# One copy of an input matrix read through a strided view instead of loaded, in two buffers: the input stage of an S5 recurrence

## The chip, the cores and the metric

The kernel runs on one core of a Trainium2 chip. The metric is the device time of one execution in microseconds. A core has five engines with a queue of instructions each: PE (matrix products, with PEld for its weight loads), DVE (vector), ACT (scalar functions), POOL (general vector work) and SP, which here issues all DMA transfers. Instructions of one queue run in the order in which they were written down. An instruction that waits holds up all that stand behind it on its engine.

## The reference

The model is a two-layer backbone over 128 context tokens and 2048 sample tokens of width 1024. Layer 0 runs an HGRN2 recurrence and an S5 recurrence side by side between an input and an output projection; layer 1 is a gated short convolution between two projections. What matters here is the input side of S5. For each of 32 groups of 16 channels and each of two directions, a complex diagonal state of 64 numbers is driven by the channels:

```python
bb_re = coef_re[..., None] * b_re - coef_im[..., None] * b_im
bb_im = coef_re[..., None] * b_im + coef_im[..., None] * b_re
bu_re = jnp.einsum('blgs,gps->blgp', useq, bb_re[d])
bu_im = jnp.einsum('blgs,gps->blgp', useq, bb_im[d])
```

and the state follows x_t = lambda x_(t-1) + bu_t.

## The kernel before

The kernel does not step through the tokens one by one. It works on blocks of 16 tokens: `s5_in` builds, for each direction and group, matrices that carry the 16 tokens of a block to the block's share in the state. It multiplies them with the channel inputs, and `s5_scan` then runs the recurrence over the blocks. `s5_out` makes the outputs.

`s5_in` has 8 rounds `r` of 4 groups. A round has two steps, one for each direction `d`. A step loads `pb` (L613: real and imaginary part of B, and beside them the same with the two parts swapped, 4 KB on each of 128 partitions, 512 KB in all). For each half `hh` of the block it loads `pe` (L617: powers of the decay times the coefficient, 2 KB on each partition, 256 KB) and makes the complex product in four instructions: DVE multiplies the real part of `pe` with `pb[:, 0]` into `psi` (L622), POOL multiplies the imaginary part with the swapped `pb[:, 1]` into `ptb` (L623), and DVE subtracts and adds the halves (L624, L625). After both steps PE multiplies the four matrices `psi` with the inputs `su` (L599, four loads of 136 KB in a round) into the PSUM tile `lv` (L633, 32 products in a round, 16 for each step), and ACT and DVE copy `lv` into the state array `sX` (L638, L639).

`pe`, `ptb`, `psi` and `su` have two buffers each, `pb` has one: the next `pb` can be loaded only when both POOL products that read the last one have ended. The source patterns of `pb` and of `pe` have 8 as their outermost size. The loads `su` also begin with 8.

Beside this stage PE works on large input projections (`pj`, L362: three products for each tile of weights, since every factor is split in a high and a low part). Their weights `wraw` come by L339, ACT and DVE or POOL split them (`whi` L342, `wlo` L346), and their outputs go through `zst` (L390, L392, L407) to DRAM.

The order of the instructions of each queue is not written by hand. The program gives each instruction a priority (`s5_in` ranks 500 ahead of what stands beside it), and a planner walks through the program before the run with an estimated duration for each instruction and transfer. Whenever an engine is free in that plan it takes the ready instruction of the highest rank. What comes out is a fixed order on each queue. How many `pj` products stand between two groups of `lv` products thus follows from how long the planner thinks that a step of `s5_in` lasts.

Of the kernel before, what the change touches and what calls it, by code (L numbers as in the profile page):

```python
# [11 lines left out]
F32 = mybir.dt.float32  # L12
# [4 lines left out]
OP = mybir.AluOpType  # L17
# [47 lines left out]
def vw(t, off, dims):  # L65
    return bass.AP(t.tensor, t.offset + off, [list(t.ap[0])] + [list(d) for d in dims])


def raw_ap(t, off, dims):
    return bass.AP(t.tensor, t.offset + off, [list(d) for d in dims])  # L70
# [525 lines left out]
def s5_load_u(nc, g, p, g0):  # L596
    u = p.tile([128, 2, NC8], F32, name="su")
    for j in range(2):
        nc.sync.dma_start(u[:, j], raw_ap(g.u_d, (g0 + j) * 16 * 8 * NC8, [(NC8, 8), (8 * NC8, 16), (1, NC8)]))  # L599
    return u  # L600


def s5_in(nc, g, p, X):

    V, A, T, G = nc.vector, nc.scalar, nc.tensor, nc.gpsimd
    W = WX
    for r in range(8):
        G0 = 4 * r
        us = [s5_load_u(nc, g, p, G0 + 2 * q) for q in range(2)]
        SI = []  # L610
        for d in range(2):
            bt = p.tile([128, 2, 4, 2, 64], F32, name="pb", bufs=1)
            nc.sync.dma_start(bt.rearrange("p a g r q -> p a (g r q)"),  # L613
                              raw_ap(g.I["s5_bt"], d * 16 * 8192 + r * 1024, [(0, 8), (8192, 16), (1, 1024)]))
            for hh in range(2):
                e = p.tile([128, 4, 2, 64], F32, name="pe")
                nc.sync.dma_start(e.rearrange("p g r q -> p g (r q)"),  # L617
                                  raw_ap(g.et_d, ((d * 16 + 8 * (1 - hh)) * 32 + G0) * 128,
                                         [(32 * 128, 8), (0, 16), (1, 512)]))
                si = p.tile([128, 4, 2, 64], F32, name=f"psi{d}{hh}")  # L620
                tb = p.tile([128, 4, 2, 64], F32, name="ptb")
                V.tensor_tensor(si, vw(e, 0, [(128, 4), (0, 2), (1, 64)]), bt[:, 0], op=OP.mult)  # L622
                G.tensor_tensor(tb, vw(e, 64, [(128, 4), (0, 2), (1, 64)]), bt[:, 1], op=OP.mult)  # L623
                V.tensor_tensor(si[:, :, 0], si[:, :, 0], tb[:, :, 0], op=OP.subtract)  # L624
                V.tensor_tensor(si[:, :, 1], si[:, :, 1], tb[:, :, 1], op=OP.add)  # L625
                SI.append(si)
        for q in range(2):
            pr = 2 * r + q
            for j in range(2):
                P = g.ps_l.tile([128, 512], F32, name="lv")  # L630
                for d in range(2):
                    for hh in range(2):
                        T.matmul(out=P[:, d * NC16:(d + 1) * NC16],  # L633
                                 lhsT=SI[2 * d + hh][:, 2 * q + j].rearrange("p r q -> p (r q)"),
                                 rhs=vw(us[q], j * NC8 + hh, [(2, NC16)]), start=(hh == 0), stop=(hh == 1))
                o = slice(64 * j, 64 * j + 64)
                Pv = P[:, :2 * NC16].rearrange("p (d a b) -> p d b a", d=2, b=8)
                A.activation(vw(X[o], pr * W + NG16, [(32 * W - NG16, 2), (NG16, 8), (1, NG16)]), Pv[0:64], AF.Copy)  # L638
                V.tensor_copy(vw(X[o], (16 + pr) * W + NG16, [(32 * W - NG16, 2), (NG16, 8), (1, NG16)]), Pv[64:128])  # L639
# [446 lines left out]
def kernel(ctx: ExitStack, tc: tile.TileContext, I, O, dram=None):  # L1086
# [118 lines left out]
    with tc.tile_pool(name="big0", bufs=1) as b0:  # L1205
        with tc.tile_pool(name="kt", bufs=1) as kt:
# [25 lines left out]
            with tc.tile_pool(name="s5x", bufs=1) as xp:  # L1232
                X = xp.tile([128, 2, 2, 16, WX], F32, name="sX")
                with tc.tile_pool(name="s5i", bufs=2) as p5:
                    with rank(tc, -RI):
                        s5_in(nc, g, p5, X)
                proj_all(nc, g, rest, p0, hs, 1)
                with tc.tile_pool(name="s5s", bufs=2) as p5:
                    with rank(tc, -RC):
                        s5_scan(nc, g, p5, X)  # L1240
                make_h(p1[0])
                with tc.tile_pool(name="s5o", bufs=2) as p5:
                    with rank(tc, -RO):
                        s5_out(nc, g, p5, X)
                nc.sync.dma_start(O["st_s5"], g.xfin)
# [113 lines left out]
def layout(inputs):  # L1359
    a = {k: np.asarray(v) for k, v in inputs.items()}  # L1360
    c = np.ascontiguousarray
    r = {}
    r["x"] = c(np.concatenate([a["x_prompt"][0], a["x_sample"][0]], 0).T)
    r["w_mod"] = c(a["w_mod"].reshape(2, 8, 128, 6, 512).transpose(0, 3, 2, 1, 4))

    def blocks(w, k):
        n = w.shape[1] // 128
        return c(w.reshape(k, 128, n, 128).transpose(2, 1, 0, 3))

    r["w_in_even"] = blocks(a["w_in_even"][0], 8)  # L1370
    r["w_out_even"] = blocks(a["w_out_even"][0], 8)
    r["w_in_odd"] = blocks(a["w_in_odd"][0], 8)
    r["w_out_odd"] = blocks(a["w_out_odd"][0], 8)
    r["w_glu"] = c(a["w_glu"][0].reshape(4, 128, 512).transpose(1, 0, 2))

    def feat(v):
        return v.reshape(-1, 128).T

    pv = np.zeros((128, PVW), np.float32)

    def put(k, v):
        pv[:, PV[k][0]:PV[k][1]] = v

    put("cvec", np.stack([a["c_ctx"], a["c"][0]], -1).reshape(8, 128, 2).transpose(1, 0, 2).reshape(128, 16))
    put("b_mod", np.concatenate([feat(a["b_mod"][l]) for l in range(2)], 1))
    put("norm_g", np.concatenate([feat(a["norm_g"][l]) for l in range(2)], 1))
    put("fin_g", feat(a["final_norm_g"]))
    put("lbl", np.concatenate([feat(a["lb_logits"][l]) for l in range(2)], 1))
    put("hg", feat(a["hgrn_norm_g"][0]))
    put("bglu", feat(a["b_glu"][0]))  # L1390
    put("convw", np.concatenate([feat(a["conv_w"][0, j]) for j in range(3)], 1))
    put("convb", feat(a["conv_b"][0]))
    d = np.zeros((4, 32, 8), np.float32)
    d[:, :16, :] = a["s5_d"][0].reshape(8, 4, 16).transpose(1, 2, 0)
    put("s5d", d.reshape(128, 8))
    r["pv"] = pv
    r["eye"] = np.eye(128, dtype=np.float32)
    e16 = np.zeros((4, 32, 16), np.float32)
    e16[:, :16] = np.eye(16)
    r["eye16"] = e16.reshape(128, 16)  # L1400
    idx = np.arange(32)
    m = np.zeros((4, 32, 6, 32), np.float32)
    m[:, :, 0] = np.eye(32)
    for l in range(5):
        h = 1 << l
        b, t = idx // (2 * h), (idx // h) % 2
        m[:, :, l + 1] = (b[:, None] == b[None]) & (t[:, None] != t[None])
    m = m.reshape(128, 6, 32)
    r["masks"] = m
    r["state_hgrn"] = c(a["state_hgrn"][0, 0].transpose(0, 2, 1, 3).reshape(2, 128, 512))  # L1410
    x0 = np.stack([a["state_s5_re"][0, 0], a["state_s5_im"][0, 0]], 1)
    r["s5_x0"] = c(x0.reshape(2, 2, 16, 2, 64).transpose(3, 4, 0, 1, 2).reshape(128, 2, 2, 16))
    r["s5_lam_re"] = c(a["s5_lam_re"][0].reshape(64, 64))
    r["s5_lam_im"] = c(a["s5_lam_im"][0].reshape(64, 64))
    r["s5_log_dt"] = c(a["s5_log_dt"][0].reshape(64, 1))
    bre, bim = a["s5_b_re"][0], a["s5_b_im"][0]
    cre, cim = a["s5_c_re"][0], a["s5_c_im"][0]
    bt = [np.stack([p, q], 2).transpose(0, 4, 1, 2, 3).reshape(2, 16, 8, 512) for p, q in ((bre, bim), (bim, bre))]
    r["s5_bt"] = c(np.stack(bt, 3))
    br, bi = bre.transpose(2, 0, 1, 3), bim.transpose(2, 0, 1, 3)  # L1420
    r["s5_x1"] = c(np.concatenate([br, bi], 0))
    r["s5_x2"] = c(np.concatenate([bi, br], 0))
    cs = np.stack([cre, cim], 1).transpose(4, 0, 1, 2, 3).reshape(64, 2, 2, 512)
    r["s5_c"] = c(np.concatenate([cs, cs], 0))
    return r
# [25 lines left out]
```

## Time and profile before

| | us |
|---|---|
| median of 3 runs | 2525.39 |
| range of the runs | 2523.67 to 2532.09 |
| the profiled execution, its own time | 2521.9 |
| span of the profile | 2520.1 |
| PE busy | 2336.8 (93%) |
| DVE busy | 1384.5 (55%) |
| ACT busy | 992.5 (39%) |
| POOL busy | 686.9 (27%) |

The profile is of one execution, and its span is 1.8 us shorter than that execution's own time. PE's clock has two levels, 1.2 and 2.4 GHz; the profile gives the mean granted clock of a stretch as a share of the higher one, so 0.81 means that a part of the stretch ran at half speed. Busy shares are means over stages with different limits. The stages can be told apart by time: modulation and the first projections up to 150 us, loads and matrices of `s5_in` beside projections to 250, the rest of `s5_in` to 391, `s5_scan` to 516, then `s5_out`, HGRN2, the output projections and layer 1.

### The profile page before, as it was taken

Reading aid. Unit: us, or ns where it says so; the run is one execution under the profiler, and the core shown is the slowest. Engines: PE = TensorE matmul, PEld = TensorE weight load, DVE = VectorE, ACT = ScalarE, POOL = GpSimd, SP = SyncE. Lnnn points to the kernel's source line nnn. Section 1 sums busy time; section 2 is a strip of 40 time slices with the busy share of each in tenths; the row PEclk is TensorE's granted clock in tenths of the full one; section 3 lists DMA queues with packets and bytes.
Section 4 is the critical chain, followed back from the end, with each engine's and each line's share of the span. In section 5 each row is a group of like instructions: output and inputs, shape, how many; then the busy total and the mean of one; then the engine's idle time right before and its main releaser. Section 6 shows DMA issues by size and latency. Waiting matters only on the chain. (4 is left out here: it accounts for less than half of the span.)

```text
span 2520.1 us, 46630 instructions
## 1 busy us (share of the span) xinstructions
PE 2336.8 (93%) x18452; PEld 2235.7 (89%) x18452; DVE 1384.5 (55%) x2960; ACT 992.5 (39%) x1991; POOL 686.9 (27%) x740
## 2 busy tenths in 40 slices
PE   5999778999989889999898999999999999999997
PEld 3998768998877778979788999999999999899997
DVE  5976648966555886067667652244622244622233
ACT  3544212234455875266444332233422232422221
POOL 0334332232222333133222322223322222322120
PEclk8999889999999989999998999999999999999999
DMA  7577653355565554453896432234321223222221
GB/s 257 149 216 216 172 157 112 117 164 156 146 196 160 156 169 153 153 182 103 249 288 214 135 113 76 76 94 140 97 68 59 65 86 115 71 67 60 67 66 60
DMA packets 277418, 340.16 MB, mean 135 GB/s; under 512 B 79056, under 2 KB 221136, under 8 KB 277072
## 3 DMA queue, kind: packets, MB, share of 16 engines
q1 hardware_dynamic: 277200, 337.18, 44.2%
q8 instruction: 145, 2.38, 0.4%
q14 instruction: 73, 0.60, 0.1%
HBM read 265.18 MB, written 71.94 MB: 134 GB/s over the span
## 5 line engine op out<-in xcount | busy, mean ns | idle before, releaser
L362 PE MATMUL pj<-hhi,whi 128*128 128x384 f32 (+1 forms) x3648 | 1178.1, 333 | 41.4 <-ACT hhi L304 24.0
L362 PE MATMUL pj<-hlo,whi 128*128 128x384 f32 (+1 forms) x3648 | 1179.8, 332 | 9.5 <-DVE hlo L305 7.8
L362 PE MATMUL pj<-hhi,wlo 128*128 128x384 f32 (+1 forms) x3456 | 1142.9, 331 | 0.3 <-DVE wlo L346 0.3
L362 PEld LDWEIGHTS pj<-hhi,whi 128*128 128x128 f32 x3648 | 691.6, 191 | 53.9 <-ACT hhi L304 25.7
L362 PEld LDWEIGHTS pj<-hlo,whi 128*128 128x128 f32 x3648 | 692.2, 191 | 17.0 <-DVE hlo L305 11.9
L362 PEld LDWEIGHTS pj<-hhi,wlo 128*128 128x128 f32 x3456 | 660.6, 191 | 3.8 <-issue 1.6
L346 POOL TENSOR_TENSOR wlo<-wraw,whi 128x256 fp32r<-128x256 f32 x472 | 382.9, 843 | 1017.5 <-ACT whi L342 948.3
L342 ACT ACTIVATE whi<-wraw 128x512 fp32r<-128x512 f32 x472 | 271.7, 623 | 560.9 <-PE pj L362 359.7
L346 DVE TENSOR_TENSOR wlo<-wraw,whi 128x256 fp32r<-128x256 f32 x472 | 191.1, 462 | 102.3 <-ACT whi L342 102.1
L1055 DVE TENSOR_TENSOR ccg<-ccg,pj 128x384 f32<-128x384 f32 (+1 forms) x48 | 25.5, 532 | 248.5 <-PE pj L362 233.0
L828 POOL TENSOR_TENSOR hK<-hK,ht 128x512 f32<-128x512 f32 x68 | 91.7, 1350 | 224.0 <-ACT hMg L812 143.1
L995 DVE SCALAR_TENSOR_TENSOR xr<-pj,mod,xr 128x384 f32<-128x384 f32 (+2 forms) x152 | 77.3, 529 | 135.5 <-PE pj L362 122.9
L304 ACT ACTIVATE hhi<-nsq,mod 128x384 fp32r<-128x384 f32 (+2 forms) x144 | 75.0, 557 | 66.3 <-DVE nsq L302 66.2
L283 DVE TENSOR_TENSOR nac<-nac,nsq 128x384 f32<-128x384 f32 (+1 forms) x112 | 71.7, 641 | 28.3 <-ACT nsq L282 25.8
L830 DVE TENSOR_TENSOR hQ<-hQ,ht 128x512 f32<-128x512 f32 x102 | 78.8, 787 | 14.8 <-PE lv L798 10.8
L623 POOL TENSOR_TENSOR ptb<-pe,pb 128x512 f32<-128x512 f32 x32 | 53.5, 1681 | 115.2 <-DMA pb<-in_s_bt 85.5
L633 PE MATMUL lv<-su,psi 128*128 128x136 f32 x256 | 47.8, 344 | 37.1 <-DVE sX L639 21.3
L305 DVE SCALAR_TENSOR_TENSOR hlo<-nsq,mod,hhi 128x384 fp32r<-128x384 f32 (+2 forms) x144 | 81.3, 591 | 1.0 <-ACT hhi L304 0.9
L282 ACT ACTIVATE nsq<-xr 128x384 f32<-128x384 f32 (+1 forms) x84 | 42.1, 503 | 96.8 <-DVE xr L995 91.3
L633 PEld LDWEIGHTS lv<-su,psi 128*128 128x128 f32 x256 | 43.2, 238 | 41.6 <-DVE sX L639 23.2
L392 ACT ACTIVATE zst<-pj 128x384 f32<-128x384 f32 (+1 forms) x96 | 44.4, 464 | 81.2 <-PE pj L362 49.6
L1075 DVE TENSOR_TENSOR ccs<-ccs,pj 128x384 f32<-128x384 f32 (+1 forms) x48 | 25.3, 528 | 88.8 <-ACT ccs L1074 88.8
(299 smaller groups left out, 2826.6 us busy)
## 6 DMA issues: line engine op xcount, KB each, us to landing
wraw<-in_w_in_odd SPq DMA_DIRECT2D x96, 512.0 KB
wraw<-in_w_in_even SPq DMA_DIRECT2D x92, 512.0 KB
mwm<-in_w_mod SPq DMA_DIRECT2D x64, 256.0 KB
big<-in_x SPq DMA_DIRECT2D x10, 1536.0 KB
wraw<-in_w_out_even SPq DMA_DIRECT2D x24, 512.0 KB
wraw<-in_w_out_odd SPq DMA_DIRECT2D x24, 512.0 KB
su<-u_d SPq DMA_DIRECT2D x64, 136.0 KB
pb<-in_s_bt SPq DMA_DIRECT2D x16, 512.0 KB
```

Of the source, the lines that this page charges most:

```text
L283: e.tensor_tensor(acc, acc, sq[:, :n], op=OP.add)
L304: A.activation(hi[:, k, a:b], raw[:, a:b], AF.Identity, bias=sh)
L305: V.scalar_tensor_tensor(lo[:, k, a:b], raw[:, a:b], sh, hi[:, k, a:b].bitcast(F32), op0=OP.add, op1=OP.subtract)
L342: nc.scalar.activation(hi[:, i:i + ca], raw[:, i:i + ca], AF.Copy)
L346: e.tensor_tensor(lo[:, k], raw[:, k], hi[:, k].bitcast(F32), op=OP.subtract)
L362: nc.tensor.matmul(out=P[:, :n], lhsT=a[:, k, :], rhs=b[:, k, :n], start=(k == 0 and i == 0), stop=(k == kd - 1 and i == 2))
L392: nc.scalar.activation(st[:, :n], P[:, :n], AF.Copy)
L623: G.tensor_tensor(tb, vw(e, 64, [(128, 4), (0, 2), (1, 64)]), bt[:, 1], op=OP.mult)
L633: T.matmul(out=P[:, d * NC16:(d + 1) * NC16], lhsT=SI[2 * d + hh][:, 2 * q + j].rearrange("p r q -> p (r q)"), rhs=vw(us[q], j * NC8 + hh, ...
L828: (G if lvl in KPOOL else V).tensor_tensor(kv, kv, vw(tot, n + 1, [(-n - 1, 2), (2, nb), (0, h)]), op=OP.mult)
L830: V.tensor_tensor(qv, qv, vw(tot, 1, [(n - 1, 2), (2, nb), (0, h)]), op=OP.mult)
L995: nc.vector.scalar_tensor_tensor(x[:, a:e], P[:, a:e], g.mod[l][:, 16 + b, s:s + 1], x[:, a:e], op0=OP.mult, op1=OP.add)
```

## The change

The array in DRAM holds the real and the imaginary part of B once, not twice, and its rows become half as long. The tile `pb` becomes 2 KB on each partition instead of 4 KB, and its DMA carries 256 KB instead of 512 KB. The swapped copy is no longer loaded: POOL's product reads the one copy through a view whose middle step is negative, first the imaginary part (offset 64), then the real part. The argument `bufs=1` goes, so that `pb` takes the two buffers of its pool; the room in SBUF is the same. The number of instructions and of transfers is unchanged.

```diff
-            bt = p.tile([128, 2, 4, 2, 64], F32, name="pb", bufs=1)
-            nc.sync.dma_start(bt.rearrange("p a g r q -> p a (g r q)"),
-                              raw_ap(g.I["s5_bt"], d * 16 * 8192 + r * 1024, [(0, 8), (8192, 16), (1, 1024)]))
+            bt = p.tile([128, 4, 2, 64], F32, name="pb")
+            nc.sync.dma_start(bt.rearrange("p g r q -> p (g r q)"),
+                              raw_ap(g.I["s5_bt"], d * 16 * 4096 + r * 512, [(0, 8), (4096, 16), (1, 512)]))
...
-                V.tensor_tensor(si, vw(e, 0, [(128, 4), (0, 2), (1, 64)]), bt[:, 0], op=OP.mult)
-                G.tensor_tensor(tb, vw(e, 64, [(128, 4), (0, 2), (1, 64)]), bt[:, 1], op=OP.mult)
+                V.tensor_tensor(si, vw(e, 0, [(128, 4), (0, 2), (1, 64)]), bt, op=OP.mult)
+                G.tensor_tensor(tb, vw(e, 64, [(128, 4), (0, 2), (1, 64)]), vw(bt, 64, [(128, 4), (-64, 2), (1, 64)]),
+                                op=OP.mult)
...
-    bt = [np.stack([p, q], 2).transpose(0, 4, 1, 2, 3).reshape(2, 16, 8, 512) for p, q in ((bre, bim), (bim, bre))]
-    r["s5_bt"] = c(np.stack(bt, 3))
+    r["s5_bt"] = c(np.stack([bre, bim], 2).transpose(0, 4, 1, 2, 3).reshape(2, 16, 4096))
```

## Rows read from the trace of the kernel before

**Rows 1.** The page, its head: busy time and instructions of each engine.
```profile
span 2520.1 us, 46630 instructions
...
PE 2336.8 (93%) x18452; PEld 2235.7 (89%) x18452; DVE 1384.5 (55%) x2960; ACT 992.5 (39%) x1991; POOL 686.9 (27%) x740
```

**Rows 2.** Stretches: length, busy of PE, PEld, DVE, ACT, POOL, PE clock, DMA share, GB/s.
```profile
150.00:250.00 100.00, 90.73 (x535) 88.28 (x534) 69.04 (x136) 39.38 (x84) 42.19 (x42) 0.93 0.78 215
200.00:220.00 20.00, 16.47 (x83) 15.61 (x84) 14.46 (x28) 7.20 (x15) 13.04 (x12) 0.83 0.76 206
250.00:391.00 141.00, 104.06 (x532) 99.49 (x530) 77.63 (x128) 31.48 (x68) 52.51 (x38) 0.82 0.61 166
366.00:370.00 4.00, 2.79 (x17) 2.46 (x15) 3.38 (x6) 0.04 (x1) 3.33 (x2) 1.00 0.53 196
369.00:376.00 7.00, 5.97 (x39) 5.87 (x39) 1.65 (x4) 2.71 (x6) 0.37 (x1) 1.00 0.55 160
391.00:516.00 125.00, 118.24 (x674) 116.24 (x675) 119.59 (x203) 37.96 (x72) 26.89 (x25) 0.99 0.36 110
2400.00:2500.00 100.00, 100.00 (x577) 100.00 (x576) 37.19 (x78) 27.05 (x53) 18.66 (x23) 1.00 0.14 43
```

**Rows 3.** Waits from 250 to 391 us: total us, times, longest.
```profile
POOL ptb L623 <- DMA pb<-in_s_bt: 69.4, 9, 12.1
...
DVE psi L622 <- DMA pb<-in_s_bt: 43.5, 9, 6.2
...
PE lv L633 <- DVE sX L639: 21.3, 6, 4.9
POOL ptb L623 <- DMA pe<-et_d: 17.8, 4, 8.7
DVE psi L622 <- DMA pe<-et_d: 14.9, 10, 6.0
```

**Rows 4.** Timeline of SP's queue over one step: start, us, what is issued.
```profile
367.70 0.58 SPq L617 DMA_DIRECT2D pe<-et_d  x1
369.39 0.61 SPq L613 DMA_DIRECT2D pb<-in_s_bt  x1
370.05 0.58 SPq L617 DMA_DIRECT2D pe<-et_d  x1
...
371.54 1.23 SPq L599 DMA_DIRECT2D su<-u_d  x2
```

**Rows 5.** Timeline of DVE, first products of steps: start, us, in brackets the wait.
```profile
200.69 0.69 DVE L622 TENSOR_TENSOR psi<-pe,pb 128x512 f32<-128x512 f32 x1 [5.23 <-DMA pb<-in_s_bt]
...
250.38 0.69 DVE L622 TENSOR_TENSOR psi<-pe,pb 128x512 f32<-128x512 f32 x1 [0.74 <-PE lv L633]
...
304.36 0.69 DVE L622 TENSOR_TENSOR psi<-pe,pb 128x512 f32<-128x512 f32 x1 [4.82 <-DMA pb<-in_s_bt]
...
376.06 0.69 DVE L622 TENSOR_TENSOR psi<-pe,pb 128x512 f32<-128x512 f32 x1 [5.41 <-DMA pb<-in_s_bt]
377.71 0.72 DVE L622 TENSOR_TENSOR psi<-pe,pb 128x512 f32<-128x512 f32 x1 [0.95 <-DMA pe<-et_d]
...
386.34 0.69 DVE L622 TENSOR_TENSOR psi<-pe,pb 128x512 f32<-128x512 f32 x1 [3.68 <-DMA pb<-in_s_bt]
```

**Rows 6.** Projection products (L362) alone in a stretch: length, PE busy, clock, DMA.
```profile
304.36:386.34 81.98, 36.70 (x176) 0.81 0.54 154
```

**Rows 7.** Timeline of PE: the products of one step of the stage.
```profile
370.03 2.20 PE L633 MATMUL lv<-su,psi 128*128 128x136 f32 x16 [1.25 <-DVE psi L625]
```

**Rows 8.** POOL's instructions by line: busy us, mean ns, idle before and releaser.
```profile
L828 POOL TENSOR_TENSOR hK<-hK,ht 128x512 f32<-128x512 f32 x68 | 91.7, 1350 | 224.0 <-ACT hMg L812 143.1 <-PE lv L824 63.2 <-DVE ht L833 7.0
L623 POOL TENSOR_TENSOR ptb<-pe,pb 128x512 f32<-128x512 f32 x32 | 53.5, 1681 | 115.2 <-DMA pb<-in_s_bt 85.5 <-DMA pe<-et_d 29.4
```

**Rows 9.** PE's waits from 150 to 250 us: total, times, longest.
```profile
PE nx L258 <- DVE nac L283: 4.0, 1, 4.0
```

## The prediction

> **What bounds the kernel now.** The head of the page comes first: PE is busy for 2336.8 of 2520.1 us [rows 1], so 183 us of idle PE are all that better order could win, and half clock hides some more. The second view cuts the span into stretches [rows 2]. From 250 to 391 us, the second part of the input stage of S5, PE is busy for 104.1 of 141 us and its granted clock is 0.82: it idles for 37 us and runs part of the rest at 1.2 GHz. From 391 to 516 us DVE is the bound (119.6 of 125 us busy) and PE has 118.2 us of work beside it. So the stretch in which PE is short of work is exactly the one that the change touches.
>
> The waits of that stretch say why [rows 3]. POOL waited 69.4 us and DVE 43.5 us for `pb`, against 17.8 and 14.9 us for `pe`. PE itself never waits for `pb`; it waits 21.3 us for `sX`, DVE's copy that frees a PSUM tile. That copy stands in DVE's queue behind the next step's `psi`, which stands waiting for `pb`. This is how a load becomes PE's idle time.
>
> The rhythm is seen in SP's queue and DVE's [rows 4, 5]. The first `pe` of a step goes out at 367.70, when one POOL product has freed its buffer. `pb` goes out at 369.39, when the second POOL product has freed the only buffer, and it is used at 376.06, 6.67 us later. The second `pe`, issued at 370.05, is used at 377.71, 7.66 us after. From 304.36 to 386.34 there are 7 such steps, so 11.71 us each; from 250.38 to 386.34 there are 11.
>
> What PE has to do in a step: 176 projection products in those 7 steps [rows 6], 25.1 a step, at 100/577 = 0.173 us each at full clock [rows 2], makes 4.35 us; the step's own 16 products take 2.20 us [rows 7]. Together 6.55 us of work in 11.71 us; 5.16 us a step are lost to idle time or half clock.
>
> **The change part by part.**
>
> *The second buffer.* The load of `pb` for the next step can go out while this step computes; its 6.67 us lie beside the step before. What is late next is the first `pe`: its buffer comes free when the first POOL product ends (1.68 us, [rows 8]), and then its load has to land. The new step is 1.68 us plus that load. The trace does not show a `pe` issued with no `pb` just ahead. From below: the second `pe`, queued right behind `pb`, is used 1.65 us after it (377.71 less 376.06, [rows 5]), so 256 KB cost about that much transfer, and today's 512 KB `pb` in 6.67 us would be a 256 KB load in 5.02. From above: the second `pe` today, 7.66 us. The step is then 6.70 to 9.34 us. I take the load at `pb`'s 6.67 us, near the middle, for the same loads share the way: 8.35 us.
>
> *Half the bytes.* A step moves 512 KB of `pb`, 512 KB of `pe` and 272 KB of `su` now and 1040 KB after, plus what the projections load. The price is inside the two ends above. While the loads of this stage fill the queue, the DMA share is 0.53 and 0.55 with 196 and 160 GB/s [rows 2], although more is waiting: about half of the 16 DMA engines work. The Trainium skill, page "DMA: Bandwidth & Descriptors", section "Rules for kernel authors", says that a leading dimension of 8, as in a broadcast of 8 copies, confines a transfer to at most 8 engines; the trace agrees with its 0.53. It speaks against the change, since the smaller load keeps its leading 8; what it would make of the time is the second rival.
>
> *The swapped view.* The 32 POOL products read runs of 64 numbers with a negative middle step. The nearest row is another POOL product of the same size, 128x512, that reads far shorter and also reversed pieces: 1350 ns against 1681 ns [rows 8]. So I take 0, with the ends -0.33 us (as that row) and +1.68 us (twice as long) a product; one POOL product a step lies in the chain, so the upper end is 11 x 1.68 = 18 us at most. DVE's `psi` reads as before: 0.
>
> *The order of the queues.* This decides how much of a shorter step becomes time. PE's queue is a fixed list. The planner puts as many projection products between two groups of `lv` as it thinks fit into a step, and it will think the step shorter. The trace shows only the 25.1 of now. The ends are 25.1 (nothing moved) and none. I take a cut in proportion to the step: 6.55 x 8.35/11.71 = 4.67 us of PE work in an 8.35 us step, 3.68 us lost. Products that leave this stretch run later, in the scan or behind it, where PE is full at full clock; they cost their 0.173 us and are already in the sum.
>
> *The sum.* Per step 5.16 - 3.68 = 1.48 us; times 11 steps 16.3 us. At the fast end of the load (6.70 us) the same rule gives 2.95 us lost and 24 us won, at the slow end (9.34) 4.12 lost and 11 won.
>
> Before 250 us the stage's matrices are built beside full projections, and there one wait for `pb` reaches PE: DVE stands for 5.23 us before 200.69 [rows 5], and PE's norm products behind it wait 4.0 us [rows 9]; the clock from 200 to 220 us falls to 0.83 [rows 2]. That stall should go: 4 us, with ends 0 (another load is late there) and 9 us (all idle time of the stretch from 150 to 250, [rows 2]).
>
> Nothing is added on ACT, and no wait is new. The earlier `pb` issue stands in SP's queue behind the second `pe`, whose buffer frees at the same moment, so SP gets no new block.
>
> 16.3 + 4 = 20.3 us from the profiled execution's own 2521.9 us gives 2501.6. The median of the runs is 3.5 us above that execution, and I forecast on its scale: 2505 us.
>
> **The rivals.**
>
> *Projections stay (faster).* If the planner leaves 25.1 products in a step, 8.35 us hold 6.55 us of work, 1.80 us are lost, and the win is 3.36 x 11 = 37 us, with the 4 us 41: 2484 us. For it: nothing in the program's ranks changes. Against it: a plan with earlier loads has fewer gaps to fill.
>
> *The DMA queue is the bound.* If the engines that these loads use are full through the whole step, the step shrinks only as the bytes do: 11.71 x 1040/1296 = 9.40 us, with 5.26 us of work by proportion and 4.14 lost; 1.02 x 11 = 11 us: 2514 us. For it: the share at 0.53 to 0.55 without a gap from 366 to 376. Against it: the mean of the stretch is 0.61 with projection traffic included, and the 8.35 us step asks for less than 1040 KB/160 GB/s = 6.7 us.
>
> *`pe` simply takes `pb`'s place.* The two `pe` of a step also free late, and both engines already wait 10 and 4 times for them [rows 3]. If `pe` lands no earlier than `pb` did, the step stays near 11 us and nothing shows: 2521 to 2527 us. This is also the case in which the second buffer doesn't do what it says, because SP's list issues `pb` no earlier.
>
> *The plan runs ahead of the chip (slower).* One mechanism on PE's queue between 250 and 391 us: the planner thinks the step so short that it fits almost no projection products in, while `pe` still needs 9.34 us. Then a step has only its 2.20 us of work and loses 7.14 us; (5.16 - 7.14) x 11 = -22 us: 2547 us. It decides from the point where step less work exceeds 5.16 us: fewer than 12 products a step at 9.34 us, fewer than 6 at 8.35 us. The projections moved out then fill a scan stage that is already full [rows 2].
>
> **How the numbers follow.** Chances: forecast 0.42, projections stay 0.16, DMA queue 0.14, `pe` in `pb`'s place 0.12, plan ahead of the chip 0.16. A measurement of this kernel can tell about 0.3% (7.6 us) from no change. Of the forecast 0.38 lies beyond it (the 11 us of the slow load still does, a lengthened POOL product would not), all of the second, and 0.10 of the third: faster 0.64. Same: 0.04, 0.04 and 0.10 of the fourth: 0.18. Slower: 0.16 and 0.02 of the fourth, whose reshuffled queues can also cost: 0.18. The range is 2480 to 2534 us: it takes in the forecast with both ends of the load, the projections that stay, and the milder half of the slow case; out of it lie a fast load with all projections kept (55 us) below and the full slow case above. The forecast's own range is 2492 to 2517 us.
>
> **What would show it.** Right: waits for `pb` nearly gone on POOL and DVE, `pe` the releaser of almost every step, steps of 7 to 9.4 us between first `psi`, fewer than 25 projection products a step, `s5_in` over about 35 us earlier, the 4 us wait at 200 us gone, POOL's product still near 1.68 us. Wrong: steps above 11 us; or short steps with the stretch's PE loss (idle and half clock) no smaller in sum; or a loss of the same size in another stage, where only the order of the queues differs.

## The result, and the profile after

The changed kernel takes 2483.93 us in the median of 4 runs (2480.67 to 2486.4) against 2526.65 us for the kernel before in the same session (4 runs): 0.9845 of the time, 95% interval 0.9821 to 0.987. A repeat in a later session gave 0.9861 (0.9843 to 0.9878). The forecast was 2505 us, faster: the direction was right and the time lies inside the range, but the gain of some 40 us (42.7 here, 35.8 in the repeat) is double the 20 us that the steps of the sum gave. The profiled execution took 2480.67 us with a span of 2478.9.

The page's head, answering to [rows 1]. PE has 16.4 us less busy time with the same 18452 products, so more of them ran at the full clock (the mean granted clock is 0.969 instead of 0.961). The span is 41.2 us shorter, so PE's idle time fell from 183 to 158 us.

```profile
span 2478.9 us, 46614 instructions
...
PE 2320.4 (94%) x18452; PEld 2224.6 (90%) x18452; DVE 1381.5 (56%) x2960; ACT 988.5 (40%) x1989; POOL 678.1 (27%) x740
```

Stretches of the kernel after, with the columns of [rows 2]. The second is the 11 steps from the first `psi` of round `r` = 2 to that of the last step. It took 90.56 us, where the same 11 steps took 135.96 before (250.38 to 386.34, at clock 0.81, DMA share 0.61 and 164 GB/s). The third is the scan, as full of DVE work as it was.

```profile
150.00:250.00 100.00, 91.90 (x550) 90.09 (x549) 69.90 (x138) 41.82 (x89) 41.34 (x44) 0.95 0.71 210
248.55:339.11 90.56, 73.39 (x431) 69.42 (x429) 70.12 (x117) 27.02 (x61) 41.52 (x32) 0.92 0.61 196
344.00:470.00 126.00, 118.25 (x664) 116.17 (x664) 118.27 (x200) 33.76 (x67) 28.00 (x25) 0.97 0.33 102
```

The same 11 steps before:

```profile
250.38:386.34 135.96, 100.14 (x510) 95.89 (x509) 74.61 (x122) 30.61 (x67) 49.05 (x36) 0.81 0.61 164
```

Waits of those 11 steps (total us, times, longest), answering to [rows 3]. No engine waits for `pb` any more. `pe` is what POOL waits for, and PE's wait for `sX` is down from 21.3 to 3.5 us.

```profile
POOL ptb L623 <- DMA pe<-et_d: 45.5, 16, 8.3
...
DVE psi L622 <- DMA pe<-et_d: 9.2, 9, 2.5
...
PE lv L634 <- DMA su<-u_d: 6.4, 5, 2.9
...
PE lv L634 <- DVE psi L626: 5.9, 5, 2.8
...
PE lv L634 <- DVE sX L640: 3.5, 2, 3.3
```

In the repeat POOL's wait for `pe` is 33.9 us, so this sum scatters by some 12 us between executions of the same queues.

SP's queue in the last steps, answering to [rows 4], and the first products of DVE there, answering to [rows 5]:

```profile
328.21 0.58 SPq L617 DMA_DIRECT2D pe<-et_d  x1
328.83 0.61 SPq L613 DMA_DIRECT2D pb<-in_s_bt  x1
329.49 0.45 SPq L339 DMA_DIRECT2D wraw<-in_w_in_even  x1
331.13 0.60 SPq L617 DMA_DIRECT2D pe<-et_d  x1
...
335.65 0.59 SPq L617 DMA_DIRECT2D pe<-et_d  x1
```

```profile
328.79 1.19 DVE L622 TENSOR_TENSOR psi<-pe,pb 128x512 f32<-128x512 f32 x1 [0.65 <-DMA pe<-et_d]
...
333.78 0.69 DVE L622 TENSOR_TENSOR psi<-pe,pb 128x512 f32<-128x512 f32 x1 [0.78 <-DMA pe<-et_d]
...
339.11 0.69 DVE L622 TENSOR_TENSOR psi<-pe,pb 128x512 f32<-128x512 f32 x1 [1.87 <-DMA pe<-et_d]
...
340.93 0.69 DVE L622 TENSOR_TENSOR psi<-pe,pb 128x512 f32<-128x512 f32 x1 [0.77 <-DMA pe<-et_d]
```

Each `pe` goes out when a buffer is free and is used by the next product but one. The load issued at 328.21 is used at 333.78 (5.57 us), that of 331.13, behind `pb` and a 512 KB `wraw`, at 339.11 (7.98), and that of 335.65 at 340.93 (5.28). A load of `pe` now sets the rhythm: a buffer comes free, SP issues, and the product that uses it starts later, by 4.1 to 9.5 us for the 22 loads of these 11 steps, 5.9 us in the mean (from the issue on SP to the first of the two products, DVE's or POOL's).

The projection products alone in the 11 steps (length, PE busy, clock, DMA), answering to [rows 6]: 233, or 21.2 a step. In the 11 steps before there were 304, or 27.6.

```profile
248.55:339.11 90.56, 45.93 (x233) 0.92 0.61 196
```

```profile
250.38:386.34 135.96, 66.60 (x304) 0.81 0.61 164
```

POOL's lines, answering to [rows 8]: the product through the swapped view takes 1527 ns in the mean, where the product from the loaded copy took 1681. In other executions it is 1623 ns (the repeat) and, from the loaded copy, 1631 ns (the kernel before with 16 first, below), so the view makes no difference that shows.

```profile
L829 POOL TENSOR_TENSOR hK<-hK,ht 128x512 f32<-128x512 f32 x68 | 93.3, 1373 | 242.7 <-ACT hMg L813 160.0 <-PE lv L825 73.2 <-DVE hAn L836 8.9
L623 POOL TENSOR_TENSOR ptb<-pe,pb 128x512 f32<-128x512 f32 x32 | 48.8, 1527 | 67.7 <-DMA pe<-et_d 67.5
```

PE's wait from 150 to 250 us, answering to [rows 9], is still there:

```profile
PE nx L258 <- DVE nac L283: 4.1, 1, 4.1
```

Where the 41.2 us came from is best read by cutting both spans at the same points of the work: the first `lv` product, the first scan instruction, the last one, the last copy that `s5_out` takes from `sX`, the last HGRN2 output. Each cell is the length in us, in parentheses the projection products (L362) in it. Some records can be missing, so counts differ by a few where the queues are the same.

| stretch | before | after | after, repeat | before, 16 first | after, 16 first |
|---|---|---|---|---|---|
| start to first `lv` | 245.2 | 243.4 | 242.2 | 241.2 | 240.9 |
| input stage | 153.6 (363) | 109.3 (271) | 109.0 (270) | 124.9 (363) | 96.7 (271) |
| scan | 114.0 (595) | 113.1 (594) | 113.0 (594) | 113.3 (590) | 112.9 (595) |
| `s5_out` | 203.3 (642) | 213.3 (665) | 213.6 (665) | 201.9 (647) | 206.7 (665) |
| HGRN2 | 505.5 (1482) | 501.1 (1550) | 506.9 (1550) | 506.0 (1482) | 502.3 (1550) |
| the rest | 1298.5 | 1298.7 | 1297.0 | 1294.8 | 1295.4 |
| span | 2520.1 | 2478.9 | 2481.7 | 2482.1 | 2454.9 |

(The last two columns are experiments below.) The input stage is 44.3 us shorter and has 92 projection products fewer. `s5_out` takes 23 of these and is 10 us longer. HGRN2 takes 68 and does not get longer by more than the scatter: -4.4 us, +1.4 in the repeat. The projection products of the scan, of `s5_out` and of HGRN2 after, and then before:

```profile
352.70:465.80 113.10, 106.67 (x594) 0.98 0.35 107
465.80:679.10 213.30, 127.95 (x665) 0.99 0.53 151
679.10:1180.20 501.10, 264.20 (x1550) 0.96 0.55 165
```

```profile
398.80:512.80 114.00, 106.75 (x595) 0.99 0.36 109
512.80:716.10 203.30, 123.41 (x642) 1.00 0.54 154
716.10:1221.60 505.50, 254.38 (x1482) 0.95 0.54 162
```

### The profile page after: what moved, and what is told of

The parts are those of the page before. It is cut to its first block, busy times and chain, and to the rows that moved or that the text cites. A ratio compares the mean times of both kernels' runs of the same rounds, so it can differ in the third digit from the quotient of the medians.

```text
span 2478.9 us, 46614 instructions
## 1 busy us (share of the span) xinstructions
PE 2320.4 (94%) x18452; PEld 2224.6 (90%) x18452; DVE 1381.5 (56%) x2960; ACT 988.5 (40%) x1989; POOL 678.1 (27%) x740
## 5 line engine op out<-in xcount | busy, mean ns | idle before, releaser
L362 PE MATMUL pj<-hhi,whi 128*128 128x384 f32 (+1 forms) x3648 | 1173.5, 332 | 43.3 <-ACT hhi L304 25.9
L362 PE MATMUL pj<-hlo,whi 128*128 128x384 f32 (+1 forms) x3648 | 1174.9, 331 | 7.5 <-DVE hlo L305 5.8
L362 PE MATMUL pj<-hhi,wlo 128*128 128x384 f32 (+1 forms) x3456 | 1139.8, 330 | 0.1
L362 PEld LDWEIGHTS pj<-hhi,whi 128*128 128x128 f32 x3648 | 688.3, 190 | 55.0 <-ACT hhi L304 27.8
L362 PEld LDWEIGHTS pj<-hlo,whi 128*128 128x128 f32 x3648 | 688.4, 190 | 13.8 <-DVE hlo L305 8.5
L362 PEld LDWEIGHTS pj<-hhi,wlo 128*128 128x128 f32 x3456 | 657.9, 190 | 1.8 <-POOL wlo L346 0.6
L346 DVE TENSOR_TENSOR wlo<-wraw,whi 128x256 fp32r<-128x256 f32 x472 | 186.2, 452 | 114.2 <-ACT whi L342 113.3
L831 DVE TENSOR_TENSOR hQ<-hQ,ht 128x512 f32<-128x512 f32 x102 | 82.5, 822 | 15.4 <-PE lv L799 11.4
L1076 DVE TENSOR_TENSOR ccs<-ccs,pj 128x384 f32<-128x384 f32 (+1 forms) x48 | 25.3, 527 | 89.2 <-ACT ccs L1075 89.2
L572 POOL TENSOR_TENSOR SOt<-C,L 128x544 f32<-128x544 f32 x32 | 38.0, 1186 | 121.9 <-DVE SO L573 117.3
L979 PE MATMUL pj<-hhi 128*128 128x384 f32 (+1 forms) x192 | 54.0, 358 | 18.3 <-ACT hhi L970 12.2
L813 ACT ACTIVATE hMg<-hK 128x512 f32<-128x512 f32 x85 | 55.3, 653 | 37.2 <-PE lv L799 23.9
L1071 DVE TENSOR_TENSOR cca<-cca,pj 128x384 f32<-128x384 f32 (+1 forms) x48 | 25.4, 529 | 79.9 <-PE pj L362 79.7
```

The source lines that it names most:

```text
L346: e.tensor_tensor(lo[:, k], raw[:, k], hi[:, k].bitcast(F32), op=OP.subtract)
L362: nc.tensor.matmul(out=P[:, :n], lhsT=a[:, k, :], rhs=b[:, k, :n], start=(k == 0 and i == 0), stop=(k == kd - 1 and i == 2))
L813: A.activation(vw(Mg, 0, [(h, 2), (2 * h, nb), (1, h)]), vw(KK, 0, sp), AF.Copy)
L831: V.tensor_tensor(qv, qv, vw(tot, 1, [(n - 1, 2), (2, nb), (0, h)]), op=OP.mult)
L979: T.matmul(out=P[:, :n], lhsT=w[:, k, b * 128:b * 128 + 128], rhs=x[:, :n], start=(k == 0 and j == 0), stop=(k == 3 and j == 2))
```

## The experiments

All kernels compute the reference in full; some load more than they need. The step below is the mean of the 11 steps, "lost" is the length of all 11 less 0.1733 us for each projection product and 0.1375 us for each `lv` product in it (182 to 206 of them), so idle time and half clock together. The kernel before was run again in each of the three sessions.

| kernel | ratio (95%) | median us | step us | projections a step | lost in 11 steps | DMA share |
|---|---|---|---|---|---|---|
| before | 1 | 2519.98 to 2526.65 | 12.36 | 27.6 | 55.0 | 0.61 |
| after | 0.9845 (0.9821 to 0.987) | 2483.93 | 8.23 | 21.2 | 23.0 | 0.61 |
| after, repeat | 0.9861 (0.9843 to 0.9878) | 2487.64 | 8.22 | 21.2 | 22.8 | 0.63 |
| half the bytes, one buffer | 0.9981 (0.9962 to 1.0) | 2514.66 | 10.63 | 25.3 | 40.5 | 0.56 |
| two buffers, bytes tied | 0.9894 (0.9875 to 0.9912) | 2494.35 | 9.00 | 22.0 | 30.5 | 0.63 |
| two buffers, loose load | 0.9947 (0.9927 to 0.9968) | 2503.43 | 7.85 | 20.1 | 21.7 | 0.61 |
| after, three `pe` | 0.9830 (0.9807 to 0.9854) | 2476.15 | 7.07 | 17.1 | 20.2 | 0.64 |
| after, 16 first | 0.9762 (0.9737 to 0.9787) | 2456.42 | 7.28 | 20.6 | 14.6 | 0.76 |
| after, 16 first, three `pe` | 0.9773 (0.9752 to 0.9795) | 2465.11 | 6.55 | 17.5 | 12.5 | 0.83 |
| before, 16 first | 0.9843 (0.9826 to 0.986) | 2483.83 | 9.78 | 27.3 | 27.3 | 0.74 |

**Half the bytes, one buffer.** The changed kernel with the old number of buffers: the load halves and the view is swapped, but `pb` still waits for its readers.

```diff
-            bt = p.tile([128, 4, 2, 64], F32, name="pb")
+            bt = p.tile([128, 4, 2, 64], F32, name="pb", bufs=1)
```

> The changed kernel with one buffer for pb: half the bytes without the second buffer. Theory (the buffer): the step still holds the load of pb between two POOL products, shorter only by the transfer of 256 KB, some 1.65 us, so steps near 10 us and 2505 to 2518 us, waits for pb still the largest on POOL. Rival (the bytes): steps near 8.2 us and 2484 to 2492 us.

Its 11 steps, and their waits:

```profile
249.36:366.32 116.96, 89.31 (x484) 83.70 (x483) 74.47 (x122) 28.63 (x63) 44.45 (x32) 0.88 0.56 165
```

```profile
POOL ptb L623 <- DMA pb<-in_s_bt: 56.1, 9, 9.9
...
DVE psi L622 <- DMA pb<-in_s_bt: 28.2, 9, 5.2
```

The waits for `pb` are back and the step is 10.63 us. Halving the bytes took 1.73 us off the 12.36, and the buffer takes off the other 2.40. In time the bytes alone are worth 0.2%, hardly told from nothing. Cut like the table above, its input stage is 16.7 us shorter (136.9), but `s5_out` is 11.0 us longer (214.3), and PE idles for 14.0 us of it instead of 7.2. Why was not tested, so the split is best read from the step. By the step and by the time, the buffer carries the larger part. The swapped view, which this kernel has too, costs nothing that shows.

**Two buffers, but the bytes kept.** Two full tiles of the old size would take 4 KB more on each partition, so the bytes are added by a load that nothing needs. The first form has no reader:

```diff
+            dm = p.tile([128, 512], F32, name="pdm", bufs=1)
+            nc.sync.dma_start(dm, raw_ap(g.I["s5_bt"], (1 - d) * 16 * 4096 + r * 512, [(0, 8), (4096, 16), (1, 512)]))
```

> The changed kernel with a further load of 256 KB ahead of each load of pb, into a tile that nobody reads: two buffers as after, but the 512 KB a step of before. Theory (the single buffer set the step): the wait for pb stays gone, pe remains the load that is late, steps of 8.2 to 9 us instead of 8.23 after and 11.7 to 12.4 before, time 2484 to 2496 us. Rival (the bytes on the queue of half the DMA engines set the step): steps back near 11 us, time 2510 to 2527 us.

This one missed its aim. A load without a reader is tied to no step, and the planner let all 16 run ahead: the last is issued at 259.5 us, before the first `lv` product. SP's queue of that kernel near 200 us (start, length, what is issued):

```profile
203.51 4.58 SPq L613 DMA_DIRECT2D pdm<-in_s_bt  x1
...
208.97 2.72 SPq L619 DMA_DIRECT2D pe<-et_d  x1
...
214.74 3.25 SPq L613 DMA_DIRECT2D pdm<-in_s_bt  x1
```

An issue takes 0.6 us elsewhere; what SP stands for in entries of 3 to 5 us the trace does not tell. The weights come late: ACT waits 43.8 us for `wraw` between 150 and 265 us and PE 18.2 us for `whi` (22.2 and 3.6 after the change, up to its first `lv`), and the first `lv` comes at 265.0 instead of 243.4. The 11 steps themselves then hold no extra bytes (7.85 us), so its 2503 us say nothing on bytes in the stage. The second form ties each load to its step with a POOL product of one column, and the tile has two buffers as `pb` has:

```diff
+            dm = p.tile([128, 384], F32, name="pdm")
+            nc.sync.dma_start(dm, raw_ap(g.I["s5_bt"], (1 - d) * 16 * 4096 + r * 512, [(0, 8), (4096, 16), (1, 384)]))
...
+            G.tensor_tensor(p.tile([128, 1], F32, name="pds", bufs=1), dm[:, 0:1], tb[:, 3, 1, 63:64], op=OP.mult)
```

> The changed kernel with a further load of 192 KB in each step, into a tile of two buffers that is freed by a one-column POOL product at the step's end, so that it cannot run ahead as the unread load of the first try did: 448 of the 512 KB of before, with two buffers. Theory (the single buffer set the step, bytes matter little): steps of 8.2 to 9 us in the stage from the ninth on, 2486 to 2498 us on the scale of a kernel before at 2525. Rival (the bytes share the way of pe and set the step): the 192 KB cost 1.2 us or more at each step, steps above 9.5 us, 2500 us or more.

```profile
260.13:359.09 98.96, 79.97 (x435) 75.09 (x434) 67.13 (x117) 27.88 (x61) 48.88 (x42) 0.88 0.63 196
```

With 448 of the old 512 KB a step and two buffers, the step is 9.00 us: 3.36 of the 4.13 us that the change took off are the buffer's without the bytes. The bytes, with the small POOL product that ties them, cost 0.77 us a step here. They also cost before the stage, where the first `lv` comes 11.4 us later than after the change (254.8), so in time this kernel keeps two thirds to three quarters of the gain (1.06% of 1.55 or 1.39).

**A third buffer for `pe`.** After the change `pe` is late, by the waits. If it is the bound, one more buffer shortens the step.

```diff
-                e = p.tile([128, 4, 2, 64], F32, name="pe")
+                e = p.tile([128, 4, 2, 64], F32, name="pe", bufs=3)
```

> The changed kernel with three buffers for pe instead of two. Theory (what is late after the change is pe, because its buffer frees late): its load goes out one half step earlier, the 49 us of POOL waits for pe shrink to under 25, steps of 6 to 7 us, 2470 to 2480 us. Rival (the DMA queue is full, so an earlier issue lands no earlier): waits of the same size, 2482 to 2487 us.

Waits of its 11 steps:

```profile
POOL ptb L623 <- DMA pe<-et_d: 21.2, 9, 4.8
POOL ptb L623 <- DVE psi L626: 14.7, 7, 6.5
```

POOL's waits for `pe` fall to 21.2 us (45.5 and 33.9 in the two executions of the change), and the step to 7.07 us: `pe` was what bounded the step. But DVE's sums, which free `ptb`, are late next, and the time isn't told from that of the change (the intervals overlap). The shorter step holds 17.1 projections instead of 21.2, so its loss fell by 2.8 us only. The input stage is 10.7 us shorter than after the change (98.6), of which 4.7 are 27 products that left it, while the start and the scan are 3.0 and 3.3 us longer. HGRN2, now with 1607 projection products, lasts 515.6 us: 68 more products cost it nothing, but with 125 more it is 10 us longer than before. Against that `s5_out`, with 33 products fewer than after the change, is 14.7 us shorter (198.6), so the two stages together are as long as after the change.

**Sixteen first.** The source patterns of `pb`, `pe`, `su` and of `sM`, a load of `s5_out`, begin with their size of 8 (copies or tokens) and have 16 (channels) behind it. Here 16 comes first; the 128 partitions of all matrices are permuted alike, so the products are the same sums. Applied to the kernel after:

```diff
-        nc.sync.dma_start(u[:, j], raw_ap(g.u_d, (g0 + j) * 16 * 8 * NC8, [(NC8, 8), (8 * NC8, 16), (1, NC8)]))
+        nc.sync.dma_start(u[:, j], raw_ap(g.u_d, (g0 + j) * 16 * 8 * NC8, [(8 * NC8, 16), (NC8, 8), (1, NC8)]))
...
-                              raw_ap(g.I["s5_bt"], d * 16 * 4096 + r * 512, [(0, 8), (4096, 16), (1, 512)]))
+                              raw_ap(g.I["s5_bt"], d * 16 * 4096 + r * 512, [(4096, 16), (0, 8), (1, 512)]))
...
-                                         [(32 * 128, 8), (0, 16), (1, 512)]))
+                                         [(0, 16), (32 * 128, 8), (1, 512)]))
...
-            nc.sync.dma_start(M[:, j], raw_ap(g.gs_d, (g0 + j) * 16 * 496, [(16, 8), (496, 16), (1, 384)]))
+            nc.sync.dma_start(M[:, j], raw_ap(g.gs_d, (g0 + j) * 16 * 496, [(496, 16), (16, 8), (1, 384)]))
```

> The changed kernel with the partitions of su, pb, pe and sM ordered channel by token instead of token by channel, so that the source patterns begin with 16 instead of 8 (sums run over the partitions, so the results do not change). If these loads work on half of the DMA engines as the share of 0.53 says, the share in the stage rises above 0.6 where these loads alone run, a 256 KB load takes some 0.8 us less, steps of 6.5 to 7.5 us and 2470 to 2480 us. If the share comes from something else: 0.53 again, steps of 8.2 us, 2482 to 2487 us.

```profile
246.12:326.23 80.11, 67.89 (x417) 65.00 (x416) 69.20 (x117) 25.40 (x57) 41.28 (x31) 0.96 0.76 221
```

The order of the instructions on every engine is that of the kernel after, line by line (but for 4 of PE's 18452 records, where two executions of the kernel after differ in 8); only the patterns differ. So the whole difference is how fast the loads are: DMA share 0.76 instead of 0.61, the step 7.28 instead of 8.23 us, a load of `pe` used 4.8 instead of 5.9 us after its issue, POOL's waits for `pe` 28.7 us instead of 45.5 and 33.9. The DMA packets in the two traces fit half the engines: in the 11 steps after the change, packets of 2 KB (`pe` and `pb`) were in flight for 65.5 us, most often 8 at a time, and more than 10 for only 0.1 us; with 16 first, more than 10 were in flight for 21.9 of 55.4 us. In the table of stretches, 12.6 us come from the input stage and 6.6 from `s5_out`. At 0.9762 it has the lowest time of the study (not told from the one with three `pe` below), and lies below both ranges. The same edit to the kernel before:

> The kernel before, with one buffer and 512 KB for pb, and only the partitions ordered so that these loads begin with 16. If half of the DMA engines is what makes a load of pb take 6.67 us, a step loses some 1.6 to 3 us of it: steps near 9 to 10.5 us instead of 12.4, 2490 to 2512 us, and waits for pb remain the largest on POOL. If the single buffer alone matters: steps above 11.5 us, 2518 to 2527 us.

```profile
246.45:354.06 107.61, 88.65 (x506) 84.51 (x505) 77.31 (x123) 29.61 (x65) 47.17 (x35) 0.91 0.74 209
```

```profile
POOL ptb L623 <- DMA pb<-in_s_bt: 41.9, 8, 8.1
...
PE lv L633 <- DVE sX L639: 11.8, 4, 3.7
```

Here too all five queues are those of the kernel before (but for 17 of PE's records). With one buffer and the full bytes the waits for `pb` stay, but shorter (41.9 us on POOL instead of 66.2 in the same 11 steps), since a load of `pb` is used 5.6 instead of 8.4 us after its issue, in the mean. 2483.83 us lies below the range expected, and is as good as the whole change. It also shows what a shorter step is worth where no product moves: the input stage keeps its 363 projections and is 28.7 us shorter, and HGRN2, with the same 1482, is unchanged (506.0 us).

**Both.** Sixteen first and three `pe`:

> The changed kernel with the loads that begin with 16 and three buffers for pe. If pe's late buffer is still what ends a step (28.7 us of POOL waits with 16 alone), steps of 5.5 to 6.8 us and 8 us or less off the time of the 16 alone: 2448 to 2456 us. If PE's own work and DVE are by now what a step takes (6.1 us of PE work in a step of 7.3): no change, 2455 to 2460 us.

```profile
249.89:321.96 72.07, 62.22 (x383) 59.22 (x382) 69.78 (x115) 24.68 (x56) 40.51 (x30) 0.95 0.83 234
```

The step is the shortest (6.55 us) and the loss the smallest (12.5 us), yet the time isn't better than with two `pe` and lies above both ranges: the profiled span is 8.4 us longer. The input stage is 5.1 us shorter (91.6), but the start and the scan are 3.8 and 4.5 longer. HGRN2 again holds 1607 projection products and takes 515.5 us, 13.2 more than without the third buffer, and `s5_out` is 8.3 shorter (198.4). DVE is busy for 69.8 of the 72.1 us, and POOL waits 21.3 us for its sums and only 3.5 for `pe`: DVE has become the bound of the stage.

**The change once more**, beside the last three:

> The changed kernel itself, beside the others of this call on one chip. Expected: 0.984 to 0.987 of the kernel before, 41 us span less, steps of 8.2 us.

The input stage repeats to 0.3 us and `s5_out` too. HGRN2 does not (506.9 instead of 501.1 us with the same queues), so some 6 us of the first execution's 41 are the scatter of that stage.

## Why the prediction was right, and where it was wrong

Of the signs that were named, the waits for `pb` gone, `pe` the releaser, a step of 7 to 9.4 us, fewer than 25 products in it, an input stage over 35 us earlier (46.1, at the first scan instruction) and an unchanged POOL product all came; the 4 us wait at 200 us did not go.

*The bound* was read rightly. The input stage was where PE was short of work, `pb`, loaded late into its single buffer, was the cause (the runs with 16 first show that the slow load was as much of it as the buffer), and the chain from `pb` over DVE's queue to `sX` to PE broke as described.

*The second buffer*: right in kind, and close in number partly by luck. The new step was to be 8.35 us between 6.70 and 9.34, with `pe` late; it is 8.23 us and `pe` is the releaser. But its two terms were off in opposite directions. The load was taken at 6.67 us from one step, the shortest of the 11 loads of `pb` before, which took 8.4 us from issue to use in the mean (up to 12.1); the loads of `pe` after take 5.9. The other term, 1.68 us until the buffer comes free, measures 2.3, since DVE's product reads `pe` too and ended after POOL's in 11 of 20 cases. With 0.1 us to the next issue the two make the 8.2. The buffer as the main term, and not the bytes, is shown by the two experiments that split them (2.40 and 3.36 of the 4.13 us).

*The swapped view*: right, at 0. The product takes 1527 and 1623 ns in the two executions, 1681 and 1631 ns where it reads a loaded copy, which is inside the ends taken.

*The order of the queues*: wrong, and this is the failed step. It had three faults. First, the step's whole PE work was cut in proportion (6.55 to 4.67 us), with the 2.20 us of its own `lv` products in it, which every step needs however short it is. Second, the projections were cut less than in proportion: over the 11 steps 27.6 a step became 21.2, where the rule gives 27.6 x 8.23/12.36 = 18.4. The sizes, with the 11 steps' own numbers (5.00 us lost of 12.36 before, 2.09 of 8.23 after; the prediction's 11.71 is the mean of the last 7): cutting all work in proportion would have won 18.4 us in the 11 steps (16.3 in the prediction, which had its work from the 7 steps of [rows 6]); cutting the projections alone, with the `lv` products that the trace has, wins 26.7; the 2.8 products a step that stayed beyond that make it the measured 55.0 - 23.0 = 32.0.

Third, the products that left were to cost their 0.173 us each elsewhere, "in the scan or behind it, where PE is full". The scan took none. HGRN2 took 68 of the 92, and PE is not full there: it idles for 48.5 us of that stage before and 35.9 after (42.3 in the repeat). At 0.173 us they would have cost 11.8 us there; the stage changed by -4.4, +1.4, -3.2 and -5.1 us in the four executions that hold 1550, and by -5.4 where the tied bytes left it 1564. That is why 44.3 us in the input stage, 15.9 of them only moved products, were kept almost whole. It has an end: with 125 products more, HGRN2 is 10 us longer in both kernels that hold them.

Against it stands a loss that the list of signs named only in general: `s5_out` is 10.0 us longer for 23 products, which explain 4.0. Of the rest, 4.1 us are PE's idle time there, 11.3 instead of 7.2 us: it waits 8.4 instead of 5.9 us for `sM`, whose pattern begins with 8, and 1.9 us for a `zst` copy by ACT that it did not wait for before. With 16 first the same queues give 206.7 us, so it is largely slow loads.

Together: the 32.0 us of the 11 steps are 28.4 over the whole input stage, since before and behind them another 21 products left (3.6 us) without making it shorter. HGRN2 adds 16.2 (4.4 and the 11.8 of its free products), the start 1.8, the scan 0.7, and `s5_out` takes 6.0: 41.1 us, against 20.3 forecast.

*The stall at 200 us*: wrong, but small. DVE no longer waits there for `pb`, yet PE still waits 4.1 us. DVE's queue after the change at that place:

```profile
197.38 0.69 DVE L622 TENSOR_TENSOR psi<-pe,pb 128x512 f32<-128x512 f32 x1 [0.50 <-DMA pe<-et_d]
197.98 1.51 DVE L283 TENSOR_TENSOR nac<-nac,nsq 128x256 f32<-128x256 f32 x1
199.92 0.69 DVE L622 TENSOR_TENSOR psi<-pe,pb 128x512 f32<-128x512 f32 x1 [0.42 <-DMA pe<-et_d]
200.53 1.48 DVE L283 TENSOR_TENSOR nac<-nac,nsq 128x256 f32<-128x256 f32 x1
201.94 0.41 DVE L625 TENSOR_TENSOR psi<-psi,ptb 128x256 f32<-128x256 f32 x1
202.27 0.41 DVE L626 TENSOR_TENSOR psi<-psi,ptb 128x256 f32<-128x256 f32 x1
202.61 0.41 DVE L283 TENSOR_TENSOR nac<-nac,nsq 128x256 f32<-128x256 f32 x1
```

It is busy almost throughout: the norm's additions stand between the `psi` work, and two of them take 1.5 us. ACT's next weights land no earlier than 202.23 either:

```profile
202.23 1.15 ACT L342 ACTIVATE whi<-wraw 128x512 fp32r<-128x512 f32 x2 [4.52 <-DMA wraw<-in_w_in_even]
```

So the place has three late things (`pb`, DVE's own work, the weights), and removing the wait for one uncovered the next. The first `lv` came 1.8 us earlier, not 4.

*The rivals.* "Projections stay" gave 2484 us, which is the time measured, but not by its mechanism alone: the products did not stay, they fell by a quarter, and the loss of 1.80 us a step that it gave is 2.09. It came close since the moved products found idle time. "The DMA queue is the bound" gave a step of 9.40 us; the step is 8.23, so the queue is not a bound by itself. Its half-true part is the reason it named: the loads that begin with 8 are slow. The Trainium skill, page "DMA: Bandwidth & Descriptors", section "Rules for kernel authors", says that such a leading size confines a transfer to at most that many engines. The runs agree: with 16 first and unchanged queues, the share in the 11 steps goes from 0.61 to 0.76 and from 0.61 to 0.74, the packets in flight go well beyond 8, and the time falls in both. "`pe` takes `pb`'s place" had the releaser right and its step of 11 us wrong: with two buffers and half a `pb` ahead of it, `pe` landed early enough for 8.23 us. "The plan runs ahead of the chip" did not come: 21.2 products a step are far above the 6 from which it would decide at this step. A mild form of it is seen with the third `pe` buffer, where HGRN2 takes 125 products more and is longer for it.

What stays open: how the planner comes to 21 products and not 18 (its durations were not varied), what lengthens `s5_out` with half the bytes and one buffer, and what scatters HGRN2 by 6 us between executions of the same queues.

## What to carry to other kernels

A shorter step is worth its whole length only if the instruction order fills it as before. So split a step's work into what it needs and what merely fills it, cut only the second, and ask where the work that leaves it will run: in a stage with idle PE time some of it is free, but not all that the idle time could hold. Here 68 and 82 products (11.8 and 14.2 us) cost HGRN2 nothing beside 48.5 us of idle time, and 125 (21.7 us) went with 10 us. In a full stage at least its duration is to be expected. When one load stops being late, ask which comes next and how fast it really is: beginning the source patterns with 16 instead of 8 was worth as much here as the buffer and the halved bytes together, without moving one instruction.

## What the runs showed of the hardware that was not expected

Loads whose source pattern begins with 8 ran as if on 8 of the 16 DMA engines, by the packets in flight, and below what the same queue moved with 16 first: 221 instead of 196 GB/s in the 11 steps (after) and 209 instead of 164 (before). The two gains add up only in part: 0.9845 and 0.9843 alone, 0.9762 together.

A DVE addition of 128x256 takes 0.41 us alone (up to 0.43 in the 59 of the trace after that have no POOL work beside them) and 1.1 to 1.5 us when more than 0.8 us of a POOL product of 128x512 lies beside it (10 cases), as POOL's queue of the kernel after shows beside the DVE rows above (the additions at 197.98 and 200.53):

```profile
197.57 1.65 POOL L623 TENSOR_TENSOR ptb<-pe,pb 128x512 f32<-128x512 f32 x1 [3.23 <-DMA pe<-et_d]
200.06 1.68 POOL L623 TENSOR_TENSOR ptb<-pe,pb 128x512 f32<-128x512 f32 x1 [0.84 <-DMA pe<-et_d]
```

In a stage where both engines share the elementwise work, DVE's part is thus dearer than its time alone suggests.
